# Three weight chunks of the second attention: low part by a negated copy and an accumulating transfer in place of a GpSimd subtraction

## The chip, the cores and the metric

The kernel runs on one core of a Trainium2 chip. Its time is the device time of one execution in microseconds (us); three executions are summarised by their median. Inside a core, several engines work at once, each through its own queue in order: TensorE (PE: matrix products; PEld is its weight loads), VectorE (DVE), ScalarE (ACT), GpSimd (POOL) and SyncE (SP, which here only issues transfers). Sixteen DMA engines move data between main memory and the on-chip memory SBUF. Transfers are issued by SP or by POOL; only those issued by POOL add to what lies at the destination. Line numbers (L654) are those of the kernel before.

## The reference, cut to what matters

Two decoder layers over 512 positions of width 1024, each a token mixer followed by a gated feed-forward part. The second mixer is the sparse attention whose output projection the change touches:

```python
def dsa_attention(h, w_in, q_gain, k_gain, w_uv, w_out, rel_bias):
    ...
    o = jnp.einsum('bshl,hlv->bshv', o_lat, w_uv.astype(jnp.float32))
    return o.reshape(B, S, DSA_HEADS * DSA_V_DIM).astype(h.dtype) @ w_out

def reference(x, c, ...):
    for i in range(DEPTH):
        ...
        x = x + g1 * mix
        h = rms_norm(x, norm_ffn[i]) * (1.0 + sc2) + sh2
        x = x + g2 * conv_ffn(h, ffn_w_up[i], ffn_conv_w[i], ffn_conv_b[i], ffn_w_down[i])
    return x
```

All is float32. The matrix `w_out` (1024 by 1024) is `dsa_w_out` in the inputs.

## The kernel before, in words

**Products in three parts.** PE multiplies in a rounded float32 format (`F32R`). To keep precision, each operand is split: the high part is the value rounded to that format, the low part is what rounding took away. A product is then three matmuls into the same PSUM bank, in `mm3` (L694): high weight by high data (L695), low weight by high data (L696), high weight by low data (L697). PE takes them in that order, so a step that has only its high weight stops at its second matmul.

**Weight chunks.** Weights come in chunks of 128 by 1024 floats (512 KB) out of the array `wst`. `split_order` (L559) lists all 80 chunks that are handled this way, in the order of use: among the last, `("dq", 0..15)` (query projection), `("do", 0, 0..3)` and `("do", 1, 0..3)` (output projection, first and second half of the heads), then eight `("up", 1, j, i)` of the second feed-forward part. `fetch` (L627) has SP load chunks into raw buffers (six places, tag `raw`), one ahead. `split_hi` (L636) fetches, then ACT copies the raw chunk into a `whi` tile (four places), which rounds it (L645). For the low part, a `wlo` tile (four places), there are two ways:

- `split_lo` (L649): an engine, DVE or POOL, subtracts `whi` from the raw chunk (L654).
- `split_sum` (L658): ACT copies the raw chunk with scale -1 into `wlo`, which gives the rounded chunk negated (L662). Then POOL issues a transfer that reads the same chunk from `wst` once more and adds it to the tile (L663). The raw buffer is free as soon as the copy is done.

`chunk` (L672) hands a chunk that is split to its user.

**The second attention.** `dsa_layer` goes through 16 heads. The order of work is written out by hand: the program order is what each engine runs. For head h, PE computes scores for the next head (`logits`), transposes the weights of head h (`transposed`, L2263; its results are moved by ACT for the first group and by DVE for the others) and, for every other head, multiplies them with the values (`weighted`, L2289, tile `av`). Between these, `fill(n)` (L2204) takes n steps from the generator `late_steps` (L2170), whose number per head stands in `LATE_STEPS` (L40): first the query projection for heads 12 to 15, then four groups mp of the output projection, each with chunk `("do", 0, mp)` and eight steps of three matmuls (tile `pt_o`). The last four steps of the last group come after all heads.

Small jobs that follow from these steps wait in the list `events`, and `follow(engine)` (L2208) emits those at its head that belong to the engine. After each of the four query projections, and after each group mp of the output projection, one such job is `split_both` (L2166): the next chunk of `split_order`, high part by ACT, low part by POOL. Other entries are `add_to_x` (L816: DVE adds the projection to the residual `x`). Beside them DVE runs `late_dots` (L2221), dot products for the conditioning (L723) that end in a small sum (L727), and POOL adds masks to the attention bias (`masked_bias`, L2228).

**After the heads.** `weighted` for the last pair of heads, `pair_hi` (L2329: DVE multiplies, ACT rounds) and `pair_lo`, the remaining steps and events; then `boundary` (L834): the second half of the output projection with the chunks `("do", 1, m)` (tile `pt_l`; two values of its m per chunk, the first two interleaved), the normalisation, and the first products of the feed-forward part. There, chunks are split by DVE and, further on, by `split_sum`.

Of the kernel before, what the change touches and what calls it, by code (L numbers as in the profile page):

```python
# [574 lines left out]
def kernel_body(ctx, tc, xT, wst, cst, smalls, crow, ccol, relb, outT):  # L575
    nc = tc.nc
    act, dve, pe, pool = nc.scalar, nc.vector, nc.tensor, nc.gpsimd
# [11 lines left out]
    def ptile(shape, name, tag):  # L589
        return banks.tile(shape, F32, name=name, tag=tag, bufs=nbanks[tag])  # L590
# [33 lines left out]
    def width(key):  # L624
        return 6 * P if key[0] == "dn" and key[2] < 3 else D

    def fetch(i):  # L627
        while pos["f"] <= min(i, len(order) - 1):
            k = order[pos["f"]]
            fetched[k] = chunk_raw(k, width(k))  # L630
            pos["f"] += 1

    def split_tile(name):
        return splits.tile([P, D], F32R, name=name)

    def split_hi(new=split_tile, ahead=FETCH):  # L636
        i = pos["i"]
        if i >= len(order):
            return
        fetch(i + ahead)  # L640
        k = order[i]
        n = width(k)
        raw = fetched.pop(k)
        hi = new("whi")
        act.activation(hi[:, :n], raw[:, :n], AF.Copy)  # L645
        pend_lo.append((k, n, raw, hi))
        pos["i"] += 1

    def split_lo(new=split_tile, engine=dve, n=99):  # L649
        while pend_lo and n:  # L650
            n -= 1
            k, w, raw, hi = pend_lo.pop(0)
            lo = new("wlo")
            engine.tensor_sub(lo[:, :w], raw[:, :w], hi[:, :w].bitcast(F32))  # L654
            ready[k] = (hi, lo)


    def split_sum():  # L658

        k, w, raw, hi = pend_lo.pop(0)  # L660
        lo = split_tile("wlo")
        act.activation(lo[:, :w], raw[:, :w], AF.Copy, scale=-1.0)  # L662
        pool.dma_start(lo[:, :w], wst[CH[k], :, :w], accum_op=OP.add)  # L663
        ready[k] = (hi, lo)
# [7 lines left out]
    def chunk(key, ahead=AHEAD):  # L672
        if ahead or key not in ready:
            prefetch(order.index(key) + ahead)
        return ready.pop(key)
# [1139 lines left out]
    def dsa_layer(l, first, man):  # L1815
        with ExitStack() as st:
# [37 lines left out]
            def project_steps(ps, ck):  # L1854
                whi, wlo = ck
                for k in range(KT):
                    w = slice(k * P, (k + 1) * P)
                    mm3(ps, whi[:, w], wlo[:, w], hs[k][0], hs[k][1], k == 0, k == KT - 1)
                    yield

            def q_hi(h, pt):
                qh = pp.tile([P, S], F32R, name="qh", bufs=QRING)
                ql = pp.tile([P, S], F32R, name="ql", bufs=QRING)
                q2 = group_squares(h)
                if h in FULL_Q:
                    Q[h, 0] = pp.tile([P, P], F32, name="q0", bufs=len(FULL_Q) - 2)
                    act.activation(qh[:, P:], pt[:, P:], AF.Copy)
                    act.activation(q2, pt, AF.Square)
                    act.activation(Q[h, 0], pt[:, :P], AF.Copy)
                else:  # L1870
                    act.activation(qh, pt, AF.Copy)
                    act.activation(q2, pt, AF.Square)
                Q[h] = (qh, ql)
                Q[h, 2] = q2

            def q_lo(h, pt):
                qh, ql = Q[h]
                c = slice(P if h in FULL_Q else 0, S)
                dve.tensor_sub(ql[:, c], pt[:, c], qh[:, c].bitcast(F32))
# [12 lines left out]
            def group_sum(g):  # L1892

                ps = ptile([P, S], "ssg", "z" if g < 3 else "x")
                for i in range(4):
                    pe.matmul(ps[32 * i:32 * i + 32], lhsT=ones_mean[:, :32], rhs=Q.pop((4 * g + i, 2)), start=True, stop=True)
                if g < 2:
                    sums = ip.tile([P, S], F32, name="sums", tag="qs1", bufs=3)
                else:
                    sums = raws.tile([P, D], F32, name="sums", tag="raw")[:, :S]  # L1900
                group[g] = sums
                act.activation(sums, ps, AF.Copy, scale=D / P)
                if g < 3:
                    rows = group[g, "rows"] = dp.tile([4, S], F32, name="msd", bufs=3)
                    nc.scalar.dma_start(rows, sums.rearrange("(i r) s -> i r s", r=32)[:, 0])

            def group_columns(g):

                sums = group.pop(g)
                if g < 3:  # L1910
                    ov = group.pop((g, "rows"))[0:1, 0:1]
                    nc.sync.dma_start(msq[:, 16 * g:16 * g + 16].rearrange("p (i j) -> p i j", i=4),
                                      bass.AP(tensor=ov.tensor, offset=ov.offset, ap=[[1, P], [S, 4], [P, QT]]))
                    return
                pt = ptile([P, S], "ssgT", "tr")
                for j in range(QT):
                    pe.transpose(pt[:, j * P:(j + 1) * P], sums[:, j * P:(j + 1) * P], ident)
                act.activation(msq[:, 16 * g:16 * g + 16].rearrange("p (i j) -> p i j", i=4),
                               pt.rearrange("p (j i r) -> p i j r", j=QT, i=4)[:, :, :, 0], AF.Copy)

            def q_seed(h0, h1):
                c = slice(h0 * QT, h1 * QT)
                act.activation(rq[:, c], msq[:, c], AF.Ln, bias=eps_c)
                act.activation(rq[:, c], rq[:, c], AF.Exp, scale=-0.5)

            def q_newton(h0, h1):

                c = slice(h0 * QT, h1 * QT)
                dve.tensor_mul(irq[:, c], rq[:, c], rq[:, c])
                dve.scalar_tensor_tensor(irq[:, c], msq[:, c], EPS, irq[:, c], op0=OP.add, op1=OP.mult)  # L1930
                dve.scalar_tensor_tensor(rq[:, c], irq[:, c], 3.0, rq[:, c], op0=OP.subtract, op1=OP.mult)
                dve.tensor_scalar(rq[:, c], rq[:, c], -0.5 * P ** -0.5, None, op0=OP.mult)
                dve.reciprocal(irq[:, c], rq[:, c])
                act.activation(irq[:, c], irq[:, c], AF.Copy, scale=-1.0)
# [225 lines left out]
            with ExitStack() as sa:  # L2160
# [3 lines left out]
                events = []  # L2164

                def split_both():  # L2166
                    split_hi()
                    split_lo(engine=pool)

                def late_steps():  # L2170

                    g, pt = late, late_pt
                    for h in range(EARLY_Q, HEADS):
                        if h > EARLY_Q:
                            pt = ptile([P, S], "pt_q", "mm")
                            g = project_steps(pt, chunk(("dq", h), 0))
                        for left in range(KT - 3 if h == EARLY_Q else KT - 1, -1, -1):
                            next(g)
                            if not left:
                                events.extend([(act, lambda h=h, pt=pt: q_hi(h, pt)),  # L2180
                                               (dve, lambda h=h, pt=pt: q_lo(h, pt)), (act, split_both)])
                                if h == HEADS - 1:
                                    events.extend([(act, lambda: group_sum(3)), None, (act, lambda: group_columns(3)),
                                                   (act, lambda: q_seed(EARLY_Q, HEADS)),
                                                   (dve, lambda: q_newton(EARLY_Q, HEADS))])
                            yield
                    for mp in range(4):
                        whi, wlo = chunk(("do", 0, mp), 0)
                        pts = {}
                        for mi, k in OUT_STEPS if mp == 0 else [(mi, k) for mi in range(2) for k in range(4)]:  # L2190
                            if k == 0:
                                pts[mi] = ptile([P, S], "pt_o", "mm")
                            pt = pts[mi]
                            c = k * 256 + mi * P
                            mm3(pt, whi[:, c:c + P], wlo[:, c:c + P], O[k][0], O[k][1], k == 0, k == 3)
                            if k == 3:
                                events.append((dve, lambda f=mp * 2 + mi, pt=pt: add_to_x(l, 2, f, pt)))
                                if mi:
                                    events.append((act, split_both))
                            yield  # L2200

                filler = late_steps()
# [386 lines left out]
```

## Time and profile before

| what | us |
|---|---|
| median of 3 runs (lowest to highest) | 1211.62 (1211.18 to 1212.91) |
| the profiled execution | 1211.85 |
| its span, first to last instruction | 1210.1 |
| POOL subtractions L654, 18 times, shortest / median / longest | 2.387 / 2.404 / 3.374 |
| DVE subtractions L654, 39 times, median | 1.218 |
| window 790 to 820: PE / DVE / ACT / POOL busy of 30 | 29.33 / 22.40 / 22.19 / 25.71 |
| window 820 to 840: PE / DVE / ACT / POOL busy of 20 | 18.76 / 18.09 / 9.24 / 8.39 |
| window 840 to 862: PE / DVE / ACT / POOL busy of 22 | 22.00 / 20.68 / 13.46 / 2.01 |

A line of a timeline reads: start in us from the start of the span, duration in us, engine, line, operation, output tile <- input tiles, shapes, how many of them run in a row; in brackets, how long the engine stood idle before it and what released it. In a list of waits, the numbers are the total in us, how many times, and the longest. In a list of instructions of one line, the three durations are shortest, median and longest in ns, followed by the first and the last start in us. The line "DMA to landing" gives the time from the issue of a transfer to its landing (shortest, median, longest, in us). A row of a window gives its length, then for PE, PEld, DVE, ACT and POOL the busy time with the number of instructions, then PE's granted clock, the share of DMA time and GB/s. The profile takes one execution; durations of matmuls overlap, so the pace is read from their starts.

### The profile page before, as it was taken

The numbers are of one execution on the slowest core, as the hardware profiler recorded it, in microseconds if no ns is written. First come the engines' busy times: TensorE is split into PE (matmuls) and PEld (weight loads), VectorE is DVE, ScalarE is ACT, GpSimd is POOL, SyncE is SP. The second block draws the span as 40 slices with busy tenths as digits, with TensorE's granted clock in tenths as the row PEclk, the third lists the DMA queues.
The fourth block names the chain that finished last, engine by engine and source line by source line (L and its number), as shares of the span: only waits on it lengthen the run. The fifth ranks groups of instructions, "written<-read, shape, count | busy, mean of one in ns | idle before, by whom it ended". The sixth has DMA issues, their size and how long they took to land.

```text
span 1210.1 us, 18262 instructions
## 1 busy us (share of the span) xinstructions
PE 1202.3 (99%) x6507; PEld 1006.2 (83%) x6507; DVE 1023.9 (85%) x1736; ACT 803.7 (66%) x1386; POOL 248.9 (21%) x287
## 2 busy tenths in 40 slices
PE   9999999999999999999999999999999999999998
PEld 6888788788898998998888778777888888888887
DVE  5898888988989989999798995678989898889883
ACT  5588786468666676765657457874786677677660
POOL 0001100001111111211000457884012122112110
PEclk9999999999999999999999999999999999999999
DMA  9778897629879898896520252355498888788662
GB/s 370 256 197 234 223 244 237 208 86 229 195 206 279 227 251 225 224 285 169 189 75 18 70 152 65 87 145 168 136 236 208 227 187 205 183 183 192 153 148 87
DMA packets 80643, 225.68 MB, mean 186 GB/s; under 512 B 16668, under 2 KB 17948, under 8 KB 80552
## 3 DMA queue, kind: packets, MB, share of 16 engines
q1 hardware_dynamic: 59616, 169.16, 42.5%
q0 software_dynamic: 20912, 55.33, 25.8%
q8 instruction: 51, 0.84, 0.3%
q14 instruction: 40, 0.33, 0.1%
q10 hardware_dynamic: 24, 0.02, 0.0%
HBM read 212.62 MB, written 2.16 MB: 177 GB/s over the span
## 4 chain that ended last, share of the span: by engine, by line
PE 96%; DMA 1%; DVE 1%; POOL 1%; ACT 0%; issue 0%; SPq 0%; DVEq 0%; POOLq 0%; ACTq 0%
PE pt_d L1742 16%; PE pt_a L1654 8%; PE pt_u L1623 6%; PE pt_a L1650 6%; PE pt_d L1654 4%; PE pt_u L1627 3%; PE pt_d L1650 3%; PE pt_q L695 2%; PE pt_l L695 2%; PE pt_q L697 2%; PE pt_q L696 2%; PE pt_l L697 2%; PE pt_l L696 2%; PE pt_qk L695 2%; PE pt_qk L697 2%; PE pt_qk L696 2%
## 5 line engine op out<-in xcount | busy, mean ns | idle before, releaser
L1742 PE MATMUL pt_d<-actlo,dnhi 128*128 128x512 f32 x288 | 112.7, 391 | 0.0
L1742 PE MATMUL pt_d<-acthi,dnhi 128*128 128x512 f32 x288 | 112.6, 391 | 0.0
L1532 ACT ACTIVATE whi<-raw 128x1024 fp32r<-128x1024 f32 x72 | 75.8, 1054 | 30.0 <-PE pt_a L1654 13.5
L645 ACT ACTIVATE whi<-raw 128x1024 fp32r<-128x1024 f32 x80 | 84.2, 1052 | 2.9 <-issue 1.1
L1623 PE MATMUL pt_u<-hh,whi 128*128 128x512 f32 x320 | 75.8, 389 | 0.0
L663 POOL DMA_DIRECT2D wlo<-wst x23 | 19.9, 865 | 265.3 <-DVE hh L807 114.2
L1742 PE MATMUL pt_d<-acthi,dnlo 128*128 128x512 f32 x288 | 73.5, 390 | 0.0
L1623 PEld LDWEIGHTS pt_u<-hh,whi 128*128 128x128 f32 x320 | 60.0, 188 | 12.6 <-issue 0.2
L1544 POOL DMA_DIRECT2D wlo<-wst x37 | 32.1, 867 | 169.4 <-ACT wlo L1540 71.3
L1742 PEld LDWEIGHTS pt_d<-actlo,dnhi 128*128 128x128 f32 x288 | 54.2, 188 | 10.2
L1742 PEld LDWEIGHTS pt_d<-acthi,dnhi 128*128 128x128 f32 x288 | 54.2, 188 | 10.1
L1742 PEld LDWEIGHTS pt_d<-acthi,dnlo 128*128 128x128 f32 x288 | 53.1, 188 | 10.3
L654 POOL TENSOR_TENSOR wlo<-raw,whi 128x1024 fp32r<-128x1024 f32 x18 | 44.7, 2488 | 80.8 <-ACT whi L645 80.7
L1650 PE MATMUL pt_a<-hh,whi 128*128 128x512 f32 x228 | 61.3, 390 | 0.0
L1350 DVE TENSOR_TENSOR_SCAN mz<-mz,diag 128x768 f32<-128x768 f32 (+1 forms) x32 | 47.6, 1487 | 15.2 <-ACT mz L1344 15.0
L723 DVE SCALAR_TENSOR_TENSOR raw<-raw,cond 128x1024 f32<-128x1024 f32 x46 | 57.6, 1279 | 1.4 <-ACT cond L1168 1.3
L1654 PE MATMUL pt_a<-hh,wlo 128*128 128x256 f32 x360 | 57.4, 282 | 0.0
L1654 PEld LDWEIGHTS pt_a<-hh,wlo 128*128 128x128 f32 x360 | 53.1, 190 | 4.6
L1969 DVE CUSTOM_DVE_ANT_0 L<-z,L,cols 128x128 f32<-128x128 f32 (+3 forms) x60 | 32.4, 547 | 27.7 <-PE tr L2269 17.8
L1555 POOL DMA_DIRECT2D whi<-wst x30 | 26.0, 868 | 132.8 <-ACT whi L1552 70.3
L695 PE MATMUL pt_q<-hh,whi 128*128 128x512 f32 x128 | 51.7, 404 | 0.0
L723 DVE SCALAR_TENSOR_TENSOR ada<-ada,cond 128x1024 f32<-128x1024 f32 x41 | 49.9, 1218 | 1.2 <-DMA ada<-wst 1.1
(426 smaller groups left out, 3814.5 us busy)
## 6 DMA issues: line engine op xcount, KB each, us to landing
raw<-wst SPq DMA_DIRECT2D x215, 512.0 KB, 5.3
wlo<-wst POOLq DMA_DIRECT2D x60, 512.0 KB, 7.8
ada<-wst SPq DMA_DIRECT2D x45, 512.0 KB, 5.7
raw<-wst SPq DMA_DIRECT2D x48, 384.0 KB, 4.8
whi<-wst POOLq DMA_DIRECT2D x30, 256.0 KB, 6.1
dnlo<-wst POOLq DMA_DIRECT2D x16, 384.0 KB, 7.0
x<-xt POOLq DMA_DIRECT2D x18, 256.0 KB, 6.0
th<-relb SPq DMA_DIRECT2D x16, 256.0 KB, 3.7
```

What stands on the lines that cost most here:

```text
L645: act.activation(hi[:, :n], raw[:, :n], AF.Copy)
L654: engine.tensor_sub(lo[:, :w], raw[:, :w], hi[:, :w].bitcast(F32))
L695: pe.matmul(out, lhsT=whi, rhs=ahi, start=start, stop=False)
L696: pe.matmul(out, lhsT=wlo, rhs=ahi, start=False, stop=False)
L697: pe.matmul(out, lhsT=whi, rhs=alo, start=False, stop=stop)
L723: dve.scalar_tensor_tensor(raw, raw, 1.0, cond, op0=OP.mult, op1=OP.mult, accum_out=dst)
L1350: dve.tensor_tensor_scan(rev, rev, diag[:, b:e][:, ::-1], 0.0, OP.mult, OP.max)
L1532: act.activation(W[j, i][0], R[j, i], AF.Copy)
L1623: pe.matmul(pt[j, i], lhsT=W[j, i][0][:, k * P:(k + 1) * P], rhs=hs[k][n], start=k + n == 0, stop=False)
L1650: pe.matmul(pt[j, bank, "both"], lhsT=w[:, c0 + k * P:c0 + (k + 1) * P], rhs=a[2], start=new and k == 0, stop=False, skip_group_check=True)
L1654: pe.matmul(out, lhsT=w[:, c0 + k * P:c0 + (k + 1) * P], rhs=a[n], start=new and k + n == 0, stop=part == 1 and k == 3 and what in ("a2", ...
L1742: pe.matmul(pt["dn", i], lhsT=dn[i][part][:, k * P:(k + 1) * P], rhs=A[j0 + k][n], start=part + k + n == 0, stop=part == 1 and k == j1 - j ...
```

## The change

After group 0 of the output projection the event stays `split_both`. After groups 1, 2 and 3 it becomes `split_by_sum`, which uses `split_sum` for the low part. Nothing else differs.

```diff
                     split_hi()
                     split_lo(engine=pool)
 
+                def split_by_sum():
+                    split_hi()
+                    split_sum()
+
                 def late_steps():
...
                             if k == 3:
                                 events.append((dve, lambda f=mp * 2 + mi, pt=pt: add_to_x(l, 2, f, pt)))
                                 if mi:
-                                    events.append((act, split_both))
+                                    events.append((act, split_by_sum if mp else split_both))
                             yield
```

The helper that it calls is there already and stays as it is:

```python
    def split_sum():

        k, w, raw, hi = pend_lo.pop(0)
        lo = split_tile("wlo")
        act.activation(lo[:, :w], raw[:, :w], AF.Copy, scale=-1.0)
        pool.dma_start(lo[:, :w], wst[CH[k], :, :w], accum_op=OP.add)
        ready[k] = (hi, lo)
```

## The prediction, made before the changed kernel was run

> **What bounds the kernel now.** I read the page's first part and chain first, then the waits of TensorE (PE) from 820 us to the end, then the timelines of each engine where the three chunks are split.
>
> ```profile
> span 1210.1 us, 18262 instructions
> PE 1202.3 (99%) x6507; PEld 1006.2 (83%) x6507; DVE 1023.9 (85%) x1736; ACT 803.7 (66%) x1386; POOL 248.9 (21%) x287
> PE 96%; DMA 1%; DVE 1%; POOL 1%; ACT 0%; issue 0%; SPq 0%; DVEq 0%; POOLq 0%; ACTq 0%
> ...
> PE av L2299 <- DVE pT L2276: 1.1, 1, 1.1
> PE tr L2269 <- ACT pT L2274: 0.2, 1, 0.2
> ...
> 839.00:1206.00 367.00, 367.00 (x1857) 312.37 (x1856) 310.83 (x494) 240.24 (x360) 60.62 (x68) 1.00 0.74 179
> ```
>
> The reader is to see that PE is the bound, and that after 820 us it waits twice only. From 839 to 1206 us it is busy for all of its 367 us, so whatever delays or advances it before 839 reaches the end unchanged: there is no slack in which a delay could vanish. The change lies at 820 to 850 us, just ahead of that stretch. (The profiled execution took 1211.85 us, 1.75 around its span; the runs' median is 0.23 lower. I add to 1211.85.)
>
> **Which chunks, and when they are needed.** The 80 splits of L645 follow `split_order`. Counting back from its end (eight `up` of layer 1, then four `do` of g 1), the three splits concerned are `("do",0,3)`, `("do",1,0)` and `("do",1,1)`. POOL subtracts them here:
>
> ```profile
> 822.52 3.37 POOL L654 TENSOR_TENSOR wlo<-raw,whi 128x1024 fp32r<-128x1024 f32 x1
> 832.30 2.63 POOL L654 TENSOR_TENSOR wlo<-raw,whi 128x1024 fp32r<-128x1024 f32 x1 [6.41 <-ACT whi L645]
> 839.62 2.40 POOL L654 TENSOR_TENSOR wlo<-raw,whi 128x1024 fp32r<-128x1024 f32 x1 [4.68 <-ACT whi L645]
> ```
>
> Their first readers are the second matmuls of `mm3` (L696). The last eight `pt_o` steps are mp 3: by `LATE_STEPS[15]` two plus one plus one, and four after the heads. So the first of them, at 827.98, opens `("do",0,3)`; `boundary` then opens `("do",1,0)` with m 0 and `("do",1,1)` with m 2, 24 matmuls later.
>
> ```profile
> 827.98 0.39 PE L695 MATMUL pt_o<-ohi,whi 128*128 128x512 f32 x1
> 828.21 0.39 PE L696 MATMUL pt_o<-ohi,wlo 128*128 128x512 f32 x1
> ...
> 829.35 0.68 PE L2269 MATMUL tr<-cons,L 128*128 128x128 f32 x4
> ...
> 832.83 1.72 PE L2299 MATMUL av<-pT,vals 128*64 128x512 f32 x6
> 835.61 1.51 PE L2299 MATMUL av<-pT,vals 128*64 128x384 f32 x10 [1.07 <-DVE pT L2276]
> 837.05 0.50 PE L695 MATMUL pt_o<-ohi,whi 128*128 128x512 f32 x1
> ...
> 840.15 0.39 PE L696 MATMUL pt_l<-ohi,wlo 128*128 128x512 f32 x1
> ...
> 845.59 0.39 PE L696 MATMUL pt_l<-ohi,wlo 128*128 128x512 f32 x1
> ```
>
> The low parts are thus needed at 828.21, 840.15 and 845.59. POOL's sums end at 825.89, 834.93 and 842.02: 2.3, 5.2 and 3.6 us early. That is the margin the new path has to fit in.
>
> **What is removed.** Three POOL subtractions (8.4 us) go. They also slowed VectorE (DVE):
>
> ```profile
> 823.57 3.40 DVE L723 SCALAR_TENSOR_TENSOR raw<-raw,cond 128x1024 f32<-128x1024 f32 x1
> ...
> 832.77 2.19 DVE L727 TENSOR_TENSOR mod<-mod,sm 128x8 f32<-128x8 f32 x1
> 834.88 1.01 DVE L2276 COPY pT<-tr 128x512 f32<-128x512 f32 x2
> ...
> L723 DVE SCALAR_TENSOR_TENSOR raw<-raw,cond x46: 1212/1219/3401, 32.6 to 831.5; 128x1024 f32<-128x1024 f32 x46
> L727 DVE TENSOR_TENSOR mod<-mod,sm x10: 166/167/2191, 109.3 to 950.8; 128x8 f32<-128x8 f32 x10
> ...
> 820.51 2.37 PE L2299 MATMUL av<-pT,vals 128*64 128x512 f32 x16
> ```
>
> Both slow instructions lie beside a POOL subtraction; their medians are 1.22 and 0.17 us. The second holds back the copy at 834.88, which PE's `av` needs. The undisturbed `av` at 820.51 is followed 2.31 us later by the next matmul; from 832.83 that gives 835.14, where the trace has 837.05. **Gain: 1.91 us** on PE.
>
> **What is added.** Per chunk: one ACT copy with scale -1, one POOL issue, and a second 512 KB read of the weights that adds into SBUF. Earlier `split_sum` calls (L662, L663) have all three:
>
> ```profile
> L662 ACT ACTIVATE wlo<-raw x23: 1042/1067/1102, 72.9 to 889.8; 128x1024 fp32r<-128x1024 f32 x23
> ...
> DMA to landing us min/median/max: 6.4/8.0/9.9
> ...
> DMA to landing us min/median/max: 5.4/7.7/10.6
> ...
> 874.54 1.05 ACT L662 ACTIVATE wlo<-raw 128x1024 fp32r<-128x1024 f32 x1
> 875.89 0.90 POOL L663 DMA_DIRECT2D wlo<-wst  x1 [33.88 <-DVE hh L807]
> ...
> 820.96 1.04 ACT L645 ACTIVATE whi<-raw 128x1024 fp32r<-128x1024 f32 x1
> 821.91 0.39 ACT L2259 ACTIVATE L<-L,nm 128x128 f32<-128x128 f32 x1
> ...
> 823.51 0.60 ACT L2274 ACTIVATE pT<-tr 128x512 f32<-128x512 f32 x1 [1.12 <-PE tr L2269]
> ...
> 832.94 0.60 ACT L2327 ACTIVATE bs<-bc 128x512 f32<-128x512 f32 x1 [0.71 <-PE bc L2325]
> ...
> 845.67 0.63 ACT L755 ACTIVATE sqa<-x 128x512 f32<-128x512 f32 x1 [6.13 <-DVE x L817]
> ```
>
> The first landing line is L663's (23 transfers), the second that of L1544, the same transfer in the feed-forward stage (37). The issue follows the copy's start by 1.35 us (874.54 to 875.89).
>
> ACT: 3 x 0.95 us at its pace. At 820.96 the copy takes 821.91's place; the `exp` behind it slides to 822.86, inside the 1.12 us that ACT idles ahead of 823.51. Behind the second copy ACT idles 0.71 us ahead of 832.94, so that `bs` comes 0.24 us later, and it is used only after `av`; behind the third it idles 6.13. No cost there; without that cover, 0.95 us each. POOL's issues (0.87 us each by L663) have nothing queued behind them until 875.89. SP: a raw buffer is released by the copy instead of by POOL, so loads start up to 2.9 us earlier (825.89 against 822.96) and run beside the new transfers. That costs PE nothing directly but lengthens landings.
>
> **The walk**, with L663's median of 8.0 us. It is the value nearest in kind and shape; the ends are 6.4 and 9.9, and L1544's 5.4 and 10.6 bound it from outside. DMA load speaks for no extreme:
>
> ```profile
> 823.00:832.00 9.00, 8.83 (x49) 7.24 (x49) 8.97 (x15) 4.45 (x10) 2.90 (x1) 1.00 0.69 240
> 836.00:842.00 6.00, 6.00 (x31) 4.56 (x28) 4.40 (x6) 1.58 (x2) 2.38 (x1) 1.00 0.26 87
> 842.00:850.00 8.00, 8.00 (x37) 6.64 (x36) 6.81 (x12) 4.33 (x7) 0.01 (x1) 1.00 0.75 261
> ```
>
> The DMA shares are 0.69, 0.26 and 0.75.
> 1. `("do",0,3)`: copy 821.91, issue 823.26, landed 831.26. PE wants it at 828.21: it **waits 3.05 us**, and everything behind on PE's queue with it, the transposes at 829.35 too.
> 2. Those move to 832.40; ACT's copy of them ends some 0.6 us after, and PE's `av` comes at 835.88, now with its operands ready: next matmul at 838.19. PE stands 1.14 behind (3.05 - 1.91).
> 3. `("do",1,0)`: ACT's split follows the copy of those transposes, so 832.40 + 0.68 (their row) + 0.5 (ACT's pace for such a copy), about 833.6; negated 834.55, issued 835.9, landed 843.9. PE wants it at 840.15 + 1.14 = 841.29: it **waits 2.6**, and stands 3.75 behind.
> 4. `("do",1,1)`: the split came at 838.49, 1.44 after the end of `av` (837.05), because ACT first needs the last head's output. Now 839.63; negated 840.58, issued 841.93, landed 849.93. PE wants it at 845.59 + 3.75 = 849.34: **waits 0.6**.
>
> Behind this the next thing that could be late is DVE's chain in `boundary`, whose first step waits for PE already:
>
> ```profile
> 844.89 1.43 DVE L817 SCALAR_TENSOR_TENSOR x<-pt_l,mod,x 128x512 f32<-128x512 f32 x2 [0.33 <-PE pt_l L697]
> ```
>
> It moves with PE. During PE's third wait it works on what m 0 and m 1 have left, so it loses nothing against PE, and the feed-forward stage starts as tightly packed as before, only later.
>
> PE then stands 849.93 - 845.59 = **4.3 us** behind, for good: 1211.85 + 4.3 = **1216.2 us**. Where the last arrival decides, the delay is L1 + L3 - 11.66 (the landing times of the first and third chunk): +1.1 at 6.4, +8.1 at 9.9.
>
> The Trainium skill ("DMA: Bandwidth & Descriptors", section "Anatomy of one DMA") gives about 2.0 us plus bytes over 436 GB/s for a GpSimd-issued transfer, so by estimate 3.2 us here. By it nothing would arrive late and the change would gain 1.9 us. The trace disagrees: no accumulating 512 KB transfer landed in under 5.4 us.
>
> **Rivals.**
> - *Not slower: the transfers land in time.* PE waits nowhere if they land within 828.21 - 823.26 = 4.95 us; then only the gain is left: 1211.85 - 1.9 = 1209.9 us. For it: this stretch is less loaded than the feed-forward stage. Against: none of 60 landings was that short. It decides below a mean of 5.8 us (half of 11.66). Chance 0.10.
> - *Short landings, small loss.* At 6.4 us, the delay is 1.1: 1213.0 us; the delay passes 0.2% (2.4 us) at a mean of 7.0. For it: the middle chunk's stretch has a DMA share of 0.26. Against: the two that count fall where it is 0.69 and 0.75, with the earlier raw loads beside them. Chance 0.15.
> - *PE's clock falls after the waits.* If matmuls ran at half pace after the first wait for as long as the wait, half of 3.05 us is lost more: 1217.7; after the second too, 1219.0. Against: the granted clock is 1.00 in every row shown. The Trainium skill ("TensorE: Matmul & The Clock Gate", section "What's actually happening") says an idle window of about 3.4 us halves the clock; no run here shows it. Chance 0.12.
>
> **How the numbers follow.** The forecast has the remaining 0.63; its own range is 1213.0 to 1220.0 (6.4 to 9.9 us). The range 1212.0 to 1220.0 leaves out the first rival and landings beyond 9.9. 0.2% is about what a measurement of this kernel tells from no change. The gain alone (1.9 us) doesn't reach it, so faster gets 0.03; same takes the rest of the first rival and the second: 0.22; slower 0.75.
>
> **What would show it.** Right: new rows for PE "pt_o L696" and "pt_l L696" waiting on the transfer of L663, some 3, 2.6 and 0.6 us; landings of these three near 8 us; `av` without its 1.1 us wait on DVE; L723 and L727 at 1.22 and 0.17 us; POOL without these three L654. Wrong: landings of 5 us, or readers of these chunks later than I counted.

## The result, and the profile after

| | before | changed |
|---|---|---|
| median of 10 runs, us | 1211.63 | 1218.6 |
| lowest to highest, us | 1211.18 to 1212.91 | 1215.16 to 1222.54 |
| span of the profiled execution, us | 1210.1 | 1216.4 |
| mean granted clock of that execution | 1.000 | 0.997 |

The changed kernel takes 1.0054 times as long (95% interval 1.0039 to 1.0070), some 7 us more. It also scatters over 7.4 us, where the kernel before stays within 1.7. The scatter goes with the mean granted clock of each run: the four runs at 0.999 took 1215.16 to 1216.73 us, the six at 0.995 to 0.997 took 1218.20 to 1222.54.

PE's waits from 815 us to the end, in the changed kernel (what waited <- what it waited for: us in total, times, longest):

```profile
PE pt_l L696 <- DMA wlo<-wst: 3.1, 1, 3.1
PE pt_o L696 <- DMA wlo<-wst: 2.8, 1, 2.8
```

The wait for DVE's copy L2276 is gone (the changed kernel has four lines more, so that the same copy is L2280 there); in its place are two waits of the low-weight matmul for the new transfer. The timeline of POOL shows the three issues, the chain of waits what hangs on them (start, duration, what):

```profile
822.74 0.89 POOL L663 DMA_DIRECT2D wlo<-wst  x1 [0.69 <-ACT wlo L662]
835.35 0.87 POOL L663 DMA_DIRECT2D wlo<-wst  x1 [11.71 <-ACT wlo L662]
841.01 0.87 POOL L663 DMA_DIRECT2D wlo<-wst  x1 [4.79 <-ACT wlo L662]
```

```profile
822.74 7.87 DMA wlo<-wst
830.61 0.04 issue
830.65 0.50 PE pt_o L696
...
832.56 0.02 ACT pT L2278
...
833.05 1.05 ACT whi L645
834.10 0.95 ACT wlo L662
835.06 0.29 issue
835.35 8.20 DMA wlo<-wst
843.55 0.04 issue
843.60 0.80 PE pt_l L696
844.39 0.43 PE pt_l L697
844.82 0.43 PE pt_l L695
```

Read it downwards. The first transfer takes 7.87 us and PE goes on 0.04 us after it. The transposes behind that matmul release ACT, which only then splits the second chunk, and the second transfer, 8.20 us, holds PE again. The two landings are in series. What the forecast's sum left out stands in the last two lines: matmuls of 512 columns follow each other every 0.43 us, where 0.23 is usual. The windows of the changed kernel show why (length, busy PE, PEld, DVE, ACT, POOL, then the granted clock, DMA share, GB/s):

```profile
828.00:830.00 2.00, 0.00 (x0) 0.00 (x0) 1.97 (x5) 0.63 (x1) 0.00 (x0) 1.00 0.99 268
842.00:843.00 1.00, 0.00 (x0) 0.00 (x0) 1.00 (x3) 0.00 (x0) 0.00 (x0) 0.85 0.59 164
843.00:844.00 1.00, 0.41 (x1) 0.41 (x2) 0.67 (x2) 0.00 (x0) 0.00 (x0) 0.50 0.83 279
844.00:849.00 5.00, 5.00 (x13) 3.84 (x13) 0.00 (x0) 0.00 (x0) 0.00 (x0) 0.50 0.98 283
849.00:850.00 1.00, 1.00 (x5) 0.83 (x4) 0.00 (x0) 0.00 (x0) 0.00 (x0) 0.74 1.04 426
850.00:851.00 1.00, 1.00 (x6) 0.81 (x5) 0.00 (x0) 0.00 (x0) 0.00 (x0) 1.00 0.66 270
850.00:1210.00 360.00, 360.00 (x1817) 306.15 (x1816) 304.67 (x483) 239.74 (x359) 58.11 (x67) 1.00 0.74 177
```

During the second wait the granted clock falls to 0.50, and it comes back at about 849.5; after the first wait it had stayed at 1.00. "PE busy 5.00 of 5.00" in 844 to 849 hides the loss: only 13 matmuls ran there. From 850 on PE is as densely busy as before, only later.

The removed subtractions gave what they held back. The lines of the changed kernel for L723 and L727, and the multiplication behind them on PE:

```profile
L723 DVE SCALAR_TENSOR_TENSOR raw<-raw,cond x46: 1215/1221/1748, 32.2 to 829.6; 128x1024 f32<-128x1024 f32 x46
L727 DVE TENSOR_TENSOR mod<-mod,sm x10: 166/167/169, 108.9 to 957.2; 128x8 f32<-128x8 f32 x10
...
834.94 2.37 PE L2303 MATMUL av<-pT,vals 128*64 128x512 f32 x16
837.25 0.50 PE L695 MATMUL pt_o<-ohi,whi 128*128 128x512 f32 x1
```

The longest of L723 and L727 are 1.75 and 0.17 us, against 3.40 and 2.19 before; `av` runs through. (1.75 is the row beside POOL's mask additions; its counterpart in the kernel before takes 1.77.)

**The account of the profiled execution.** First wait 2.77, second 3.07; the slow clock: 14 matmuls from 843.60 take 6.04 us to 849.64, at 0.227 us each 3.18, so 2.86 lost; gain on `av` 1.91. That is 2.77 + 3.07 + 2.86 - 1.91 = 6.8 us. The execution stood 0.49 us earlier than the one before already at the first product of the first chunk (827.49 against 827.98), which leaves 6.3: the difference of the spans.

### The profile page after: what moved, and what is told of

Same layout as the page of the kernel before. It is cut to its first block, busy times and chain, and to the rows that moved or that the text cites. A ratio compares the mean times of both kernels' runs of the same rounds, so it can differ in the third digit from the quotient of the medians.

```text
span 1216.4 us, 18268 instructions
## 1 busy us (share of the span) xinstructions
PE 1204.8 (99%) x6507; PEld 1008.3 (83%) x6507; DVE 1019.2 (84%) x1736; ACT 807.0 (66%) x1389; POOL 242.8 (20%) x287
## 4 chain that ended last, share of the span: by engine, by line
PE 95%; DMA 2%; DVE 1%; ACT 1%; POOL 1%; issue 0%; SPq 0%; ACTq 0%; DVEq 0%; POOLq 0%
PE pt_d L1742 16%; PE pt_a L1654 8%; PE pt_u L1623 6%; PE pt_a L1650 6%; PE pt_d L1654 4%; PE pt_u L1627 3%; PE pt_d L1650 3%; PE pt_l L696 3%; PE pt_l L697 2%; PE pt_l L695 2%; PE pt_q L695 2%; PE pt_q L697 2%; PE pt_q L696 2%; PE pt_qk L695 2%; PE pt_qk L697 2%; PE pt_qk L696 2%
## 5 line engine op out<-in xcount | busy, mean ns | idle before, releaser
L663 POOL DMA_DIRECT2D wlo<-wst x26 | 22.5, 864 | 289.0 <-DVE hh L807 120.6
L1544 POOL DMA_DIRECT2D wlo<-wst x37 | 32.2, 870 | 168.9 <-ACT wlo L1540 82.2
L723 DVE SCALAR_TENSOR_TENSOR raw<-raw,cond 128x1024 f32<-128x1024 f32 x46 | 55.4, 1232 | 1.4 <-ACT cond L1168 1.3
L723 DVE SCALAR_TENSOR_TENSOR ada<-ada,cond 128x1024 f32<-128x1024 f32 x41 | 50.0, 1219 | 1.6 <-DMA ada<-wst 1.5
L654 POOL TENSOR_TENSOR wlo<-raw,whi 128x1024 fp32r<-128x1024 f32 x15 | 36.3, 2426 | 69.7 <-ACT whi L645 69.6
```

Source lines behind the costliest of these rows:

```text
L723: dve.scalar_tensor_tensor(raw, raw, 1.0, cond, op0=OP.mult, op1=OP.mult, accum_out=dst)
```

## The experiments

**Theory:** the low parts land some 8 us after their issue, later than PE wants them, and the clock falls after such a wait. **Rivals:** A, the three ACT copies delay the softmax; B, the 1.5 MB more of transfers slow other loads; C, for the scatter, that landings vary and the clock is beside the point.

### The same chunks, asked for earlier

In the changed kernel each chunk is split one event sooner, the first by half a group and the two others by a whole one; the ring of four `wlo` tiles has room for it.

```diff
-                                if mi:
+                                if (mp, mi) in ((0, 1), (1, 0), (1, 1), (2, 1)):
                                     events.append((act, split_by_sum if mp else split_both))
```

> The same three chunks by copy and transfer, each asked for one event earlier (after the first half and the end of group 1 and after group 2, instead of after groups 1, 2 and 3). Theory (PE waits because the transfers land some 8 us after their issue): all three land ahead of their readers, no wait of PE on them is left, and only the 1.9 us of the removed subtractions show: 1209.7 us, within 0.8. Rival A (the three extra ACT copies cost the time) and rival B (the extra 1.5 MB of transfers slow the other loads): copies and bytes are all still there, so 1215 to 1222 us as in the changed kernel.

Measured: 1209.31 us (1208.64 to 1210.69), ratio to the kernel before 0.9983 (0.9974 to 0.9992). Its POOL timeline:

```profile
816.86 0.89 POOL L663 DMA_DIRECT2D wlo<-wst  x1 [1.20 <-ACT wlo L662]
823.01 0.90 POOL L663 DMA_DIRECT2D wlo<-wst  x1
832.02 0.86 POOL L663 DMA_DIRECT2D wlo<-wst  x1 [8.11 <-ACT wlo L662]
```

The landings took 6.5, 9.3 and 8.0 us, 7.9 in the mean as against 8.0 in the changed kernel; the first came out shorter, but at 823.4 it is 4 us ahead of its reader at about 827.5, so that 8 us would have been in time too. From 815 us on PE waits for nothing. All copies and all bytes are there, so A and B fall as costs of their own: what costs is the place of the split. This version is faster than both kernels.

### DVE instead of POOL, in place

```diff
                 def split_by_sum():
                     split_hi()
-                    split_sum()
+                    split_lo()
```

> The same three low parts by a subtraction on DVE, in place: no POOL subtraction, no copy, no transfer. Theory (POOL's subtractions hold DVE up and cost PE 1.9 us in the kernel before): L723 and L727 fall to 1.22 and 0.17 us, PE's 1.1 us wait for the copy L2276 goes, 1209.8 us, within 0.6. Rival (the slow DVE instructions have another cause): they stay, and DVE has 3 x 1.22 us more: 1211.6 to 1213 us.

Measured: 1209.88 us (1209.44 to 1210.77), ratio 0.9986 (0.9977 to 0.9995). L727 takes 0.17 us there, and the copies start 0.09 us after its start:

```profile
832.63 0.17 DVE L727 TENSOR_TENSOR mod<-mod,sm 128x8 f32<-128x8 f32 x1
832.72 1.01 DVE L2280 COPY pT<-tr 128x512 f32<-128x512 f32 x2
```

By this version POOL's subtractions cost the kernel before some 1.5 us. DVE's three extra subtractions (1.60, 1.22 and 1.22 us) show little: PE's one new wait is 0.2 us, for ACT.

### The copies alone

The kernel before, with the negating copies ahead of POOL's subtraction, which writes over them:

```diff
                 def split_by_sum():
                     split_hi()
-                    split_sum()
+                    k, w, raw, hi = pend_lo.pop(0)
+                    lo = split_tile("wlo")
+                    act.activation(lo[:, :w], raw[:, :w], AF.Copy, scale=-1.0)
+                    pool.tensor_sub(lo[:, :w], raw[:, :w], hi[:, :w].bitcast(F32))
+                    ready[k] = (hi, lo)
```

> The kernel before with the three negating ACT copies added ahead of POOL's subtraction, which overwrites them; no extra transfer. Theory (copies lie in idle time of ACT): 1211.6 us, within 0.8. Rival A (copies cost the time): 1215 us or more.

Measured: 1210.4 us (1210.2 to 1211.88), ratio 0.9992 (0.9984 to 1.0001). A would have needed 1215. It came out below the range expected, 1.0 us under the kernel before, though the interval just reaches 1. The likely reason stands in three of its rows (DVE, POOL):

```profile
822.92 3.40 DVE L723 SCALAR_TENSOR_TENSOR raw<-raw,cond 128x1024 f32<-128x1024 f32 x1
...
832.13 0.17 DVE L727 TENSOR_TENSOR mod<-mod,sm 128x8 f32<-128x8 f32 x1
...
832.61 2.36 POOL L2175 TENSOR_TENSOR wlo<-raw,whi 128x1024 fp32r<-128x1024 f32 x1 [7.36 <-ACT wlo L2174]
```

POOL waits for the copy and starts 0.48 us after L727, which is therefore fast, and PE's wait for L2276's copy is gone as well. L723 is still slow at 3.40, and PE has no wait from it. So the gain of the change hangs on one instruction of eight columns, L727, and on when it meets the subtraction. There L723 may matter after all, though no run tests it by itself: in the kernel before DVE is busy for 8.97 of the 9 us from 823 to 832, so what L723 loses beside the first subtraction pushes L727 back, to 832.77, and the second subtraction runs from 832.30. In the changed kernel and in the version with earlier splits, where that L723 takes 1.22 us, L727 starts at 830.90.

### Small matmuls in PE's waits

The changed kernel, with matmuls on constants into an idle PSUM bank ahead of the first product of the first and of the second chunk:

```diff
+                        if mp == 3:
+                            keep_busy(20)
...
+        if n == 2:
+            keep_busy(24)
```

> The changed kernel with small matmuls on constants into an idle bank ahead of the first and second chunk's first product (20 and 24 of them, some 2.2 and 2.7 us), so that PE has work in most of both waits. Theory (after a wait of about 3 us PE's granted clock halves for some 6 us, which costs 2.9 us in the profiled run and makes the runs spread): the clock stays at 1.00, 1215.4 us, within 1, lowest to highest under 2 us apart. Rival (spread and the rest come from landings): 1218.6 us and 1215 to 1222 as before.

Measured: 1218.86 us (1218.80 to 1220.29), clock 1.00. The size was wrong, as the rows of PE show:

```profile
827.66 4.63 PE L837 MATMUL pt_idle<-ones_r 128*128 128x128 f32 x40
...
841.72 5.52 PE L837 MATMUL pt_idle<-ones_r 128*128 128x128 f32 x48
```

Each runs as two passes, so that they outlast the waits: PE waits for no transfer, and 4.4 and 5.3 us of small matmuls (from their starts to the next product) stand in the path. The median says nothing for or against C. Nor does the scatter, 1.5 us instead of 7.4: with work that outlasts the waits, neither a varying landing nor the clock can show. So again with half of them (10 and 12):

> As busy_waits with half the small matmuls, 10 and 12: in busy_waits each ran as two passes, 4.4 and 5.3 us in all, longer than the waits. Now 2.2 and 2.6 us, inside them. Theory (the clock halves after the wait; landings set the rest): clock 1.00 in every run, PE still waits some 0.6 and 0.4 us for the transfers, 1215.4 us within 1, lowest to highest under 2 us. Rival (the spread and all of the loss come from landings): 1218.6 us, 1215 to 1222.

Measured: 1215.34 us (1214.64 to 1216.79), ratio 1.0034 (1.0021 to 1.0046). The row of the window after the second chunk's landing:

```profile
844.00:848.00 4.00, 4.00 (x20) 3.27 (x19) 0.30 (x1) 0.00 (x0) 0.00 (x0) 1.00 0.97 259
```

Twenty matmuls in 4 us, at clock 1.00, where the changed kernel had 13 in 5. The transfers are the same and work was added to PE, yet the time falls by 3.3 us and the scatter to 2.2. The one remaining wait for a transfer is 0.7 us, for the first chunk. Not all of the 3.3 us is the clock: the second transfer landed in 6.3 us here against 8.2, so that PE reads it at 842.91 instead of 843.60. Of the 3.55 us between the two profiled executions (1214.65 and 1218.20), 0.69 are this landing, and the other 2.86 are the loss to the slow clock counted above. So C does not hold as it stands: landings vary, but in the pair that can be compared the clock is four fifths of the difference, and in the changed kernel's ten runs the scatter goes with the clock. The remaining 3.7 us or so are the late landings less the gain.

### One chunk at a time

The condition reads `mp == 1`, `mp == 2` or `mp == 3` in place of `mp`; the two other chunks go back to POOL.

> Copy and transfer for the first chunk (do 0 3) alone, POOL's subtraction for the two others. Theory: PE waits 2.8 us for it, and the 1.9 us come back since POOL's second subtraction now comes after L727: 1212.4 us, 1214 at most if the clock falls. Rival (each chunk's copy, issue and bytes cost a third of the 7 us): 1213.7 us.

> Copy and transfer for the second chunk (do 1 0) alone. Theory: L727 is free of POOL (1.9 us gained), PE comes to the chunk at about 838.2 and waits for a landing at about 841.5, 3.2 us: 1212.7 us, up to 1215.6 where the clock halves after the wait. Rival (a third of the loss each): 1213.7 us.

> Copy and transfer for the third chunk (do 1 1) alone, which PE doesn't wait for in the changed kernel. Theory: with no earlier wait to hide behind, it lands at about 848.8 and is wanted at 845.6: a wait of 3.2 us on pt_l L696 that the changed kernel doesn't have, L727 stays slow: 1214.6 us, up to 1217.5 with the clock. Rival (a third each): 1213.7 us; rival (it costs nothing, as in the changed kernel's trace): 1211.5 us.

| chunk | median, us | lowest to highest | ratio (interval) | landing | PE's wait |
|---|---|---|---|---|---|
| first | 1214.49 | 1213.74 to 1215.87 | 1.0025 (1.0014 to 1.0035) | 8.7 | 3.6 |
| second | 1215.42 | 1214.37 to 1217.30 | 1.0034 (1.0022 to 1.0046) | 8.8 | 3.9 |
| third | 1215.11 | 1213.46 to 1219.61 | 1.0038 (1.0024 to 1.0052) | 9.4 | 4.5 |

The last columns are from the profiled executions, for the first and the third by these rows of PE's waits:

```profile
PE pt_o L696 <- DMA wlo<-wst: 3.6, 1, 3.6
```

```profile
PE pt_l L696 <- DMA wlo<-wst: 4.5, 1, 4.5
PE av L2303 <- DVE pT L2280: 1.1, 1, 1.1
```

Each chunk alone costs 3 to 4 us, together they cost 7: no thirds of the 7. The third chunk shows it best. In the changed kernel PE never waits for it, because PE is late already when it lands; alone it is waited for 4.5 us in the profiled execution, and the old wait for the copy is there too, since L727 meets the second subtraction (2.19 us) again. First and second came out above what was expected, 1214.5 and 1215.4 against 1212.4 and 1212.7, the first above the 1214 allowed for the clock as well: by landings 0.7 to 0.8 us longer than 8 and by the clock, which falls in both profiled executions and stays at half for some 3.4 us, about 1.7 us of loss. The windows of the first, with 8 matmuls in 2 us in the middle one; PE went on at 831.86, so the fall comes after the wait:

```profile
832.00:834.00 2.00, 2.00 (x9) 1.63 (x10) 0.00 (x0) 0.00 (x0) 0.00 (x0) 0.72 0.78 258
834.00:836.00 2.00, 2.00 (x8) 1.60 (x7) 0.00 (x0) 1.54 (x2) 0.00 (x0) 0.50 0.11 45
836.00:838.00 2.00, 2.00 (x14) 1.59 (x14) 1.51 (x3) 0.16 (x1) 1.98 (x1) 0.93 0.00 0
```

The eight runs of the third fall apart by their mean granted clock: four at 1.000, from 1213.46 to 1214.57 us; one at 0.998 at 1215.64; three at 0.997 or 0.998, from 1218.76 to 1219.61. The same kernel on the same chip thus pays the clock in some executions and not in others.

## Why the prediction was right, point by point

- **PE as the bound, nothing absorbed later:** right. PE is busy 360 of 360 us from 850 on, and the delay at the third chunk's reader (851.93 against 845.59, 6.34) is the difference of the spans.
- **Which chunks, and when they are needed:** right; the waits are on the very rows named, `pt_o` and `pt_l` L696.
- **Removed subtractions, 1.9 us:** right as a sum (`av` runs through; 1.0 to 2.1 us between medians in the three versions without that meeting and without a wait for a transfer). Of the two slow instructions, L727 is the one that PE waits for; L723 at 3.40 gives PE no wait where L727 is fast.
- **ACT copies at no cost:** right, by the copies alone.
- **Landing 8.0 us:** 7.9, 8.2 and 7.9 in the changed kernel. The estimate of 3.2 us quoted there from the Trainium skill ("DMA: Bandwidth & Descriptors", section "Anatomy of one DMA") is not borne out here: none of the changed kernel's 26 transfers of L663 landed in under 6.4 us.
- **Waits of 3.05, 2.6 and 0.6:** 2.77, 3.07 and none. The first two make the sum nearly what was forecast. The third was to be 0.6 us, and the second wait's extra 0.47 us and the shorter third landing are enough to remove it: PE comes to the third chunk at 851.93, without the 2.86 us of slow clock it would be 849.07, and the chunk landed at 848.9.
- **The clock:** named as a rival at 0.12, with 1217.7 to 1219.0 as its time, and the fall of the clock is what happened. This is the mis-sized term: the forecast had it at zero, and it measured 2.86 us in the profiled execution. The rival's size was luck: it charged half of each of two waits, 2.8 us in all, where the trace has one fall, after one wait, for 6.8 us. With PE kept busy, the clock at 1.00, the median is 1215.3, 0.9 us from the forecast of 1216.2. The argument against it, "1.00 in every row shown", was no evidence, since PE's longest wait in the kernel before is 1.1 us, with no wait of 3 us beside which the clock could have fallen.
- **The range, 1212.0 to 1220.0:** it was drawn for landings of 6.4 to 9.9 us. The landings came near 8, and the clock used up the room meant for longer ones; two of the ten runs (1222.12 and 1222.54) lie above it. That the median lies inside is in part luck.

## What to carry to other kernels

Ask of every low part, copy or load not what it costs but how long before its reader it is issued: replacing a 2.4 us instruction that sits 2.3 us ahead of its reader by a chain of 1 us and 8 us needs an earlier place, and with that place the same change gained 2 us instead of losing 7. Late arrivals don't add up by count: they act in series where one wait delays the next issue, and a later one hides behind an earlier one. Price a wait of some 3 us or more on a PE that is otherwise dense above its length, because the clock may fall during it or just after.

## What the runs showed of the hardware that was not expected

The clock fell during a wait of 3.07 us, and not in one of 2.77 in the same execution; it stayed at 0.50 for 6.8 us (842.7 to 849.5), longer than the wait. The Trainium skill ("TensorE: Matmul & The Clock Gate", section "What's actually happening") gives half clock after an idle window of about 3.4 us that runs freely. The trace agrees on the half; a shorter wait was enough here. The lengths of the falls agree with it too: 6.8 us in the changed kernel, 3.4 with the first chunk alone (832.9 to 836.3), 3.4 with the second (842.6 to 846.0), 6.8 with the third (848.4 to 855.2), so once or twice 3.41 us each time. With the first and the second alone the clock fell 1.0 and 1.1 us after the wait had ended.

One reading fits these four traces. Lay stretches of 3.41 us end to end, back from each fall: in the stretch just before the fall PE is busy for 1.02 to 1.45 us, and in every other stretch that holds a part of a wait, where the clock stayed, for 1.80 or more. By that, the place of a wait in such stretches would decide along with its length, and the same wait would be paid in some executions and not in others. The stretches are laid out from the falls that they are to explain, and no run moved a wait on purpose, so this stays a reading.

A POOL subtraction slows some DVE instructions for its whole duration, down to one of eight columns (0.17 to 2.19 us), while the copies out of PSUM behind L727 ran at their usual 1.01 us for two beside one (version with the copies alone, 832.21 beside 832.61).
